# Two hybrid decoder layers: the gate and up products of the feed-forward past column 512 with the weights stationary and all tokens moving

## The chip, the core and the metric

The kernel runs on one core of a Trainium2 chip. The metric is the device time of one execution in microseconds (us). A time "at" a point of the program is counted from the start of the profiled span.

TensorE multiplies a stationary operand (`lhsT`, at most 128 by 128, brought in by a LDWEIGHTS instruction, PEld in the profile) by a moving one (`rhs`, here 128 rows and up to 512 columns) and adds into a PSUM bank. The result's partitions are the stationary operand's columns, its free dimension is the moving operand's columns. So which of the two operands is stationary decides how the result lies.

## The reference

A trunk of two layers over 256 tokens of width 1024, float32. Each layer is feed-forward, three causal mixers side by side, feed-forward:

```python
def swiglu(h, w_gate, w_up, w_down):
    return (jax.nn.silu(h @ w_gate) * (h @ w_up)) @ w_down
...
x = x + 0.5 * swiglu(rms_norm(x, ffn_norm[l, 0]), ...)   # D_MODEL 1024, D_FF 2816
...
x = x + jnp.concatenate([ya, yb, yc], axis=-1) @ w_out[l]
x = x + 0.5 * swiglu(rms_norm(x, ffn_norm[l, 1]), ...)
```

The change touches the four feed-forwards alone, and in them the way from the normed input to the hidden activations `silu(gate) * up`.

## The kernel before

**Numbers.** A product in float32 is made of three matmuls in TensorE's float32r type. Each factor is split in two parts that add up to it: `hi` (a cast on ScalarE, L173 for weights, L194 for activations) and `lo` (the rest, a subtraction on VectorE, L174 and L195). `mm3` (L187 to L191) adds x_hi*w_hi, x_hi*w_lo and x_lo*w_hi.

**Weights** come from HBM in units of 128 x 1024 float32 (512 KB): `unit` issues the DMA on SP's queue into one of 3 `raw` buffers, then makes `hi` and `lo`, of which there are 7 buffers each. For a block of 512 columns a unit holds two of the eight slices of 128 input features (k), so gate and up take four units each. For 256 columns a unit holds four slices.

**One feed-forward** (`ffn`, L255). `norm` is called once for each tile of 128 tokens: it scales x by the norm's weight, transposes it on TensorE (L225) and splits it into `xh` and `xl` (features on partitions, 8 slices k, 256 tokens). The tokens' factors `rs[t]` (one number per token, its power taken on GpSimd, L219) are not multiplied in there but left for the products. Then a loop goes over the 2816 columns in five blocks of 512 and one of 256. In a block, for each token tile t, the 128 tokens are stationary and the weights move: 24 matmuls into `pg`, 24 into `pu`, each [128 tokens x 512 features] in its own PSUM bank. ScalarE makes `sg = silu(rs*pg)` (L286), VectorE `sg = (rs*pu)*sg` (L287). Since the next product needs features on partitions, `late()` transposes `sg` on TensorE, four times 128 by 128 (two times in the last block; L293), and splits the result into `hth` and `htl`. `late()` of one token tile is called between the gate and the up products of the next.

**The down product** (`down`, L229) has the hidden activations stationary and w_down moving, in 22 steps of 12 matmuls over four PSUM banks. It adds to x (L253); its last four steps go tile by tile so that the next norm can begin.

**What sets the order.** The code is written as one stream; the Tile framework schedules each engine's instructions, so that an instruction may stand before others that the code has earlier. In each engine's queue the order is fixed. PSUM's eight banks are shared by all tiles. The first feed-forward, the mixers of layer 0, two feed-forwards, the mixers of layer 1 and the last feed-forward follow each other. In the mixers, `proj_f` (L306) already multiplies with weights stationary: 128 features stationary, the 256 tokens moving (L314 to L316).

Of the kernel before, what the change touches and what calls it, by code (L numbers as in the profile page):

```python
# [10 lines left out]
F32 = mybir.dt.float32  # L11
# [5 lines left out]
L = 256  # L17
# [22 lines left out]
# columns of the constants  # L40
# [9 lines left out]
# columns of a layer's small parameters  # L50
# [55 lines left out]
class K:  # L106
    def __init__(self, ctx, tc, I, out):
# [9 lines left out]
        per = self.cp.tile([128, 2 * D + NC_CONST + 2 * L + 128], F32, name="per")  # L117
# [4 lines left out]
        self.zero = per[:, o + 2 * L:]  # L122
# [38 lines left out]
    # ---- weights: float32 as two parts that add up to it exactly  # L161
# [35 lines left out]
    # ---- norm and transpose: x[t] -> xn^T as two parts  # L197
# [7 lines left out]
    # defer: the tokens' factors are left for the products (returned)  # L205
# [48 lines left out]

    def ffn(self, l, f):  # L255
# [4 lines left out]
        rs = [self.norm(0, prep, True)]  # L260
        first = self.units([wg[:512, 0:512]], 4, 2)
        if l == 0 and f == 0:
            self.load(1)
        rs.append(self.norm(1, prep, True))
        hh, hl = [], []
        late = lambda: None
        for c0 in range(0, FF, 512):
            cw = min(512, FF - c0)
            nb = cw // 128
            per = 1024 // cw  # L270
            ug = self.units([wg[:, c0:c0 + cw]], 8, per) if c0 else first + self.units([wg[512:, 0:512]], 4, 2)
            uu = self.units([wu[:, c0:c0 + cw]], 8, per)
            ht = self.s4([4, L], "hth", F32R)
            lt = self.s4([4, L], "htl", F32R)
            hh.append(ht)
            hl.append(lt)
            for t in range(2):
                ts = slice(t * 128, (t + 1) * 128)
                pg, pu = self.mm()[:, :cw], self.mm()[:, :cw]
# [10 lines left out]
                def late(nb=nb, cw=cw, ts=ts, sg=sg, ht=ht, lt=lt):  # L290
                    tp = self.tp()
                    for b in range(nb):
                        T.transpose(tp[:, b * 128:(b + 1) * 128], sg[:, b * 128:(b + 1) * 128], self.ident)  # L293
                    self.split(ht[:, :nb, ts], lt[:, :nb, ts], tp[:, :cw].rearrange("p (k c) -> p k c", k=nb))
# [6 lines left out]
        self.down(lhs, wd, range(FF // 128), 0.5, late)  # L301

    # ---- w_in: columns c0:c0+n, features on partitions, all tokens
# [15 lines left out]
    # the second half of the tokens is normed when first needed  # L319
# [5 lines left out]
    # tokens on partitions  # L325
# [14 lines left out]
    # ---- (I + low)^-1 of eight heads, by blocks; lts: low^T[s, h, t] of four heads each; res: the inverses' transposes  # L340
    def inverse(self, lts, res):
# [38 lines left out]
        # 32 -> 64  # L380
# [21 lines left out]
        # 64 -> 128  # L402
# [15 lines left out]
    # (I + low) W = R, four heads  # L418
# [8 lines left out]
    # y[tokens, n*128] -> columns k0.. of the two parts of y^T  # L427
# [9 lines left out]
    def rwkv(self, l, w, xn):  # L437
# [4 lines left out]
        def pre():  # L442
# [58 lines left out]
            # cumulative log decay, centred within each tile  # L501
# [13 lines left out]
            # keys  # L515
# [639 lines left out]
```

## Time and profile before

| | us |
|---|---|
| device time, median of 3 runs | 1194.26 |
| lowest and highest of them | 1193.89, 1194.32 |
| span of the profiled execution, first to last instruction | 1192.2 |
| busy in it: PE, DVE, ACT | 1139.2, 720.7, 559.3 |
| mean granted clock of TensorE, share of full speed | 0.974 |

No time of the profiled execution other than its span is given; the 2.1 us between the span and the median lie around it. How to read the rows: a matmul's duration on PE holds its way through the array, and matmuls overlap, so what a matmul takes of PE is the distance from one start to the next, not its duration. The busy time of PE counts overlaps once. A row that ends in `[0.50 <-ACT hi L173]` says that the engine was idle for 0.50 us before it, and what ended that. "x2" at a row's end means two instructions merged into one row.

### The profile page before, as it was taken

Reading aid. Unit: us, or ns where it says so; the run is one execution under the profiler, and the core shown is the slowest. Engines: PE = TensorE matmul, PEld = TensorE weight load, DVE = VectorE, ACT = ScalarE, POOL = GpSimd, SP = SyncE. Lnnn points to the kernel's source line nnn. Section 1 sums busy time; section 2 is a strip of 40 time slices with the busy share of each in tenths; the row PEclk is TensorE's granted clock in tenths of the full one; section 3 lists DMA queues with packets and bytes.
Section 4 is the critical chain, followed back from the end, with each engine's and each line's share of the span. In section 5 each row is a group of like instructions: output and inputs, shape, how many; then the busy total and the mean of one; then the engine's idle time right before and its main releaser. Section 6 shows DMA issues by size and latency. Waiting matters only on the chain. (4 is left out here: it accounts for less than half of the span.)

```text
span 1192.2 us, 20036 instructions
## 1 busy us (share of the span) xinstructions
PE 1139.2 (96%) x8100; PEld 947.5 (79%) x8100; DVE 720.7 (60%) x1206; ACT 559.3 (47%) x859; POOL 103.7 (9%) x136
## 2 busy tenths in 40 slices
PE   6999999998889999999999999999987999999998
PEld 5778887896678887888887878879866888888887
DVE  5554645689865745555465456457989366554642
ACT  5444544574463544444344445346743544443531
POOL 1000000114312100000000000001233020000000
PEclk9999999999969999999999999999999699999999
DMA  8666765652210365667646657655412105666661
GB/s 285 186 189 189 209 199 144 181 162 72 74 38 20 114 193 164 189 192 232 183 135 190 181 162 243 195 149 165 140 55 74 37 19 144 187 194 182 197 198 64
DMA packets 96988, 182.59 MB, mean 153 GB/s; under 512 B 9856, under 2 KB 36608, under 8 KB 96896
## 3 DMA queue, kind: packets, MB, share of 16 engines
q1 hardware_dynamic: 96752, 181.25, 50.9%
q8 instruction: 63, 1.03, 0.3%
q14 instruction: 29, 0.24, 0.1%
q10 hardware_dynamic: 144, 0.07, 0.0%
HBM read 180.25 MB, written 1.05 MB: 152 GB/s over the span
## 5 line engine op out<-in xcount | busy, mean ns | idle before, releaser
L174 DVE TENSOR_TENSOR lo<-raw,hi 128x1024 fp32r<-128x1024 f32 (+2 forms) x332 | 407.2, 1230 | 333.0 <-ACT hi L173 318.5
L173 ACT CAST hi<-raw 128x1024 fp32r<-128x1024 f32 (+2 forms) x332 | 346.9, 1047 | 405.2 <-PE mm L191 231.1
L189 PE MATMUL mm<-hi,xh 128*128 128x512 f32 (+2 forms) x896 | 338.2, 381 | 1.2 <-ACT xh L194 0.7
L191 PE MATMUL mm<-hi,xl 128*128 128x512 f32 (+2 forms) x896 | 337.3, 376 | 2.0 <-DVE xl L195 2.0
L190 PE MATMUL mm<-lo,xh 128*128 128x512 f32 (+2 forms) x896 | 338.0, 377 | 0.9 <-DVE lo L174 0.9
L190 PEld LDWEIGHTS mm<-lo,xh 128*128 128x128 f32 x896 | 170.4, 190 | 36.4 <-DVE lo L174 6.8
L191 PEld LDWEIGHTS mm<-hi,xl 128*128 128x128 f32 x896 | 170.1, 190 | 34.4 <-DVE xl L195 3.4
L189 PEld LDWEIGHTS mm<-hi,xh 128*128 128x128 f32 x896 | 168.7, 190 | 35.5 <-ACT hi L173 4.5
L189 PE MATMUL mm<-hi,hth 128*128 128x512 f32 x352 | 139.1, 395 | 0.0
L190 PE MATMUL mm<-lo,hth 128*128 128x512 f32 x352 | 138.7, 394 | 0.0
L191 PE MATMUL mm<-hi,htl 128*128 128x512 f32 x352 | 138.4, 393 | 0.0
L191 PEld LDWEIGHTS mm<-hi,htl 128*128 128x128 f32 x352 | 66.1, 188 | 15.6
L189 PEld LDWEIGHTS mm<-hi,hth 128*128 128x128 f32 x352 | 66.1, 188 | 15.2
L190 PEld LDWEIGHTS mm<-lo,hth 128*128 128x128 f32 x352 | 66.1, 188 | 15.0
L315 PE MATMUL mm<-xl,hi 128*128 128x256 f32 x208 | 59.3, 285 | 0.2 <-DVE xl L195 0.2
L314 PE MATMUL mm<-xh,hi 128*128 128x256 f32 x208 | 59.0, 284 | 0.1
L316 PE MATMUL mm<-xh,lo 128*128 128x256 f32 x208 | 58.9, 283 | 0.0
L219 POOL TENSOR_TENSOR ss<-ss,per 128x1 f32<-128x1 f32 x12 | 10.3, 857 | 516.0 <-DVE ss L218 502.1
L286 ACT ACTIVATE sg<-mm,ss 128x512 f32<-128x512 f32 (+1 forms) x48 | 31.3, 653 | 26.2 <-PE mm L191 26.2
L195 DVE TENSOR_TENSOR htl<-tp,hth 128x512 fp32r<-128x512 f32 (+1 forms) x48 | 31.0, 645 | 17.9 <-ACT hth L194 17.9
L314 PEld LDWEIGHTS mm<-xh,hi 128*128 128x128 f32 x208 | 39.7, 191 | 0.9 <-ACT xh L194 0.5
L315 PEld LDWEIGHTS mm<-xl,hi 128*128 128x128 f32 x208 | 39.9, 192 | 0.6 <-DVE xl L195 0.6
(314 smaller groups left out, 1220.3 us busy)
## 6 DMA issues: line engine op xcount, KB each, us to landing
raw<-in_ffn_w_gate SPq DMA_DIRECT2D x88, 512.0 KB, 4.5
raw<-in_ffn_w_up SPq DMA_DIRECT2D x88, 512.0 KB, 4.5
raw<-in_ffn_w_down SPq DMA_DIRECT2D x88, 512.0 KB, 4.2
raw<-in_w_in SPq DMA_DIRECT2D x46, 512.0 KB, 3.9
raw<-in_w_out SPq DMA_DIRECT2D x16, 512.0 KB, 3.6
gb<-in_ffn_norm SPq DMA_DIRECT2D x4, 512.0 KB, 3.9
raw<-in_w_in SPq DMA_DIRECT2D x4, 384.0 KB, 3.4
pp<-in_params SPq DMA_DIRECT2D x2, 729.5 KB, 4.8
```

The costliest lines, as they stand in the source:

```text
L173: self.A.copy(hi[:, :n], raw[:, :n])
L174: self.V.tensor_tensor(lo[:, :n], raw[:, :n], hi[:, :n].bitcast(F32), op=OP.subtract)
L189: T.matmul(ps, lhsT=x[0], rhs=w[0], start=first, stop=False)
L190: T.matmul(ps, lhsT=x[0], rhs=w[1], start=False, stop=False)
L191: T.matmul(ps, lhsT=x[1], rhs=w[0], start=False, stop=last)
L195: self.V.tensor_tensor(lo, src, hi.bitcast(F32), op=OP.subtract)
L219: G.tensor_tensor(ss[:, 3:4], ss[:, 2:3], self.c("pwr")[:, 0:1], op=OP.pow)
L286: A.activation(sg, pg, AF.Silu, scale=rs[t])
L314: T.matmul(o, lhsT=h, rhs=xh[:, k, :], start=k == 0, stop=False)
L315: T.matmul(o, lhsT=h, rhs=xl[:, k, :], start=False, stop=False)
L316: T.matmul(o, lhsT=l, rhs=xh[:, k, :], start=False, stop=k == 7)
```

## The change

Block 0 (the first 512 columns) keeps tokens stationary, but its four groups of 24 matmuls come in another order: gate for tile 0 and tile 1, then up for tile 0 and tile 1 (before: gate and up for tile 0, then for tile 1). Its two `late()` are called after the gate products of block 1.

From block 1 on, 128 columns of the weights are stationary and all 256 tokens move. A PSUM bank holds two groups of 128 features by 256 tokens; a block of 512 has two banks for gate and two for up. Gate runs over all of its four units, then up over its four. The result has features on partitions, as the down product needs it, so nothing is transposed there. But the tokens' factors lie along the free dimension now: `spread` makes them a tile `rsb` [128 x 256] with the same row in each partition, by two plain float32 matmuls of a 128 x 128 matrix of ones with a diagonal of the factors (`dg`). VectorE multiplies both gate banks by it into `gr`, ScalarE takes silu in place, VectorE multiplies both up banks into `ur`, then `ur` by `gr`, and `ur` is split into `hth` and `htl`. The `late()` that `down` gets does nothing.

The core of the diff (the rest takes comment lines out and makes room for the matrix of ones):

```diff
+    def spread(self, rs):
+        V, T = self.V, self.T
+        ps = self.tp()
+        for t in range(2):
+            dg = self.sm([128], "dg")
+            V.tensor_scalar(dg, self.ident, rs[t], None, op0=OP.mult)
+            T.matmul(ps[:, t * 128:(t + 1) * 128], lhsT=self.ones, rhs=dg, start=True, stop=True)
+        rb = self.sm([L], "rsb")
+        self.A.copy(rb, ps[:, :L])
+        return rb
...
-        for c0 in range(0, FF, 512):
...
+        h0, l0 = hold()
+        acc = {}
+        for i, us in enumerate((ug, None)):
+            us = us or self.units([wu[:, 0:512]], 8, 2)
+            for t in range(2):
+                ps = acc[i, t] = self.mm()
+                for k in range(8):
+                    self.mm3(ps, (xh[:, k, t * 128:(t + 1) * 128], xl[:, k, t * 128:(t + 1) * 128]), us[k], k == 0, k == 7)
+            if i == 0:
+                rb = self.spread(rs)
...
+        lates = [turn(0), turn(1)]
+        for c0 in range(512, FF, 512):
...
-                for ps, u in ((pg, ug), (pu, uu)):
-                    for k in range(8):
-                        self.mm3(ps, (xh[:, k, ts], xl[:, k, ts]), u[k], k == 0, k == 7)
-                    if ps is pg:
-                        late()
-                sg = self.sm([512], "sg")[:, :cw]
-                A.activation(sg, pg, AF.Silu, scale=rs[t])
-                V.scalar_tensor_tensor(sg, pu, rs[t], sg, op0=OP.mult, op1=OP.mult)
...
+            for i, w in enumerate((wg, wu)):
+                us = self.units([w[:, c0:c0 + cw]], 8, 1024 // cw)
+                pp = [self.mm() for _ in range(nb // 2)]
+                acc.append(pp)
+                for k in range(8):
+                    for b in range(nb):
+                        o = pp[b // 2][:, (b % 2) * L:(b % 2 + 1) * L]
+                        h, lo = [p[:, b * 128:(b + 1) * 128] for p in us[k]]
...
+                        mm(h, xh, True)
+                        mm(h, xl, False)
+                        mm(lo, xh, False)
+                if i == 0:
+                    for late in lates:
+                        late()
...
+                for q, ps in enumerate(pp):
...
+                    V.tensor_tensor(two(g[q]), two(ps), rb[:, None, :].to_broadcast([128, 2, L]), op=OP.mult)
+                    if i == 0:
+                        A.activation(g[q], g[q], AF.Silu)
+                        sg.append(g[q])
+                    else:
+                        V.tensor_tensor(g[q], g[q], sg[q], op=OP.mult)
+                        self.split(ht[:, 2 * q:2 * q + 2, :], lt[:, 2 * q:2 * q + 2, :], two(g[q]))
```

**How it moves instructions.** In the mixers and in the down products each engine's order is the same in both kernels, but for the load of the next norm's weights on SP's queue, which stands three weight units later. Three places in the feed-forward differ. In the rows, the number behind a name tells one buffer from another.

PE, before, at the end of a group of gate products and the start of the up products (`mm_509` and `mm_510` are the gate and up banks of token tile 0 in block 2, `hi_479` and `hi_485` weight units, `tp_535` the transposes of the tile before):

```order
L191 MATMUL mm_509<-hi_479,xl_76 128x512
L189 MATMUL mm_509<-hi_479,xh_75 128x512
L190 MATMUL mm_509<-lo_480,xh_75 128x512
L191 MATMUL mm_509<-hi_479,xl_76 128x512
L293 MATMUL tp_535<-per_70,sg_456 128x128 x4
L189 MATMUL mm_510<-hi_485,xh_75 128x512
L190 MATMUL mm_510<-lo_486,xh_75 128x512
L191 MATMUL mm_510<-hi_485,xl_76 128x512
```

These four transposes stand between the two groups of 24. PE, after, at the same kind of place in block 1 (`mm_318` and `mm_319` are the two gate banks, `mm_460` the first up bank; `sg_286` and `sg_289` belong to block 0):

```order
L328 MATMUL mm_319<-xl_77,hi_314 128x256
L328 MATMUL mm_319<-xh_76,lo_315 128x256
L328 MATMUL mm_319<-xh_76,hi_314 128x256
L328 MATMUL mm_319<-xl_77,hi_314 128x256
L328 MATMUL mm_319<-xh_76,lo_315 128x256
L310 MATMUL tp_416<-per_70,sg_286 128x128 x4
L310 MATMUL tp_423<-per_70,sg_289 128x128 x4
L328 MATMUL mm_460<-xh_76,hi_438 128x256
L328 MATMUL mm_460<-xl_77,hi_438 128x256
```

Such transposes stood at each of these places; now the eight of block 0 stand here and no others follow. A feed-forward had 44 on PE and has 8. The 1536 matmuls of 512 columns in blocks 1 to 4 of the four feed-forwards are 3072 of 256.

PE, before, where token tile 0 needs its last up unit (`hi_503`, the eighth of the block) while the gate products of tile 1 (`mm_569`) use the first ones again:

```order
L190 MATMUL mm_569<-lo_468,xh_75 128x512
L191 MATMUL mm_569<-hi_467,xl_76 128x512
L189 MATMUL mm_510<-hi_503,xh_75 128x512
L189 MATMUL mm_569<-hi_473,xh_75 128x512
L190 MATMUL mm_569<-lo_474,xh_75 128x512
L191 MATMUL mm_569<-hi_473,xl_76 128x512
L189 MATMUL mm_569<-hi_473,xh_75 128x512
L190 MATMUL mm_510<-lo_504,xh_75 128x512
L191 MATMUL mm_510<-hi_503,xl_76 128x512
L189 MATMUL mm_510<-hi_503,xh_75 128x512
L190 MATMUL mm_510<-lo_504,xh_75 128x512
```

The first product with `hi_503` stands five matmuls ahead of the second. PE, after, where one unit of a block gives way to the next:

```order
L328 MATMUL mm_319<-xh_76,hi_296 128x256
L328 MATMUL mm_319<-xl_77,hi_296 128x256
L328 MATMUL mm_319<-xh_76,lo_297 128x256
L328 MATMUL mm_318<-xh_76,hi_302 128x256
L328 MATMUL mm_318<-xl_77,hi_302 128x256
L328 MATMUL mm_318<-xh_76,lo_303 128x256
L328 MATMUL mm_318<-xh_76,hi_302 128x256
L328 MATMUL mm_318<-xl_77,hi_302 128x256
```

Before, a block needs its eight units twice with seven buffers, and the scheduler set the last up unit's products in between those of the next tile. After, a unit is used in one run of 24 matmuls and is then free.

DVE, before, one and a half token tiles of blocks 1 and 2 (`lo` splits weight units, `sg` is the product with the up bank, `htl` the split of the transposed tile):

```order
L287 SCALAR_TENSOR_TENSOR sg_396<-mm_340,ss_79,sg_396 128x512
L174 TENSOR_TENSOR lo_468<-raw_465,hi_467 128x1024
L195 TENSOR_TENSOR htl_338<-tp_425,hth_337 128x4x128
L174 TENSOR_TENSOR lo_474<-raw_471,hi_473 128x1024
L174 TENSOR_TENSOR lo_480<-raw_477,hi_479 128x1024
L174 TENSOR_TENSOR lo_486<-raw_483,hi_485 128x1024
L287 SCALAR_TENSOR_TENSOR sg_456<-mm_400,ss_116,sg_456 128x512
L174 TENSOR_TENSOR lo_492<-raw_489,hi_491 128x1024
L174 TENSOR_TENSOR lo_498<-raw_495,hi_497 128x1024
L195 TENSOR_TENSOR htl_338<-tp_535,hth_337 128x4x128
L174 TENSOR_TENSOR lo_504<-raw_501,hi_503 128x1024
```

One instruction on a result stands between every one to three weight splits. DVE, after, from within the up products of block 1 to the gate products of block 2 (`mm_460` and `mm_461` are up banks of block 1, `mm_594` the first gate bank of block 2):

```order
L175 TENSOR_TENSOR lo_701<-raw_698,hi_700 128x1024
L175 TENSOR_TENSOR lo_707<-raw_704,hi_706 128x1024
L341 TENSOR_TENSOR ur_558<-mm_460,rsb_210 128x512
L341 TENSOR_TENSOR ur_559<-mm_461,rsb_210 128x512
L346 TENSOR_TENSOR ur_558<-ur_558,gr_430 128x512
L346 TENSOR_TENSOR ur_559<-ur_559,gr_431 128x512
L175 TENSOR_TENSOR lo_713<-raw_710,hi_712 128x1024
L196 TENSOR_TENSOR htl_293<-ur_558,hth_292 128x512
L196 TENSOR_TENSOR htl_293<-ur_559,hth_292 128x512
L175 TENSOR_TENSOR lo_719<-raw_716,hi_718 128x1024
L175 TENSOR_TENSOR lo_835<-raw_832,hi_834 128x1024
L175 TENSOR_TENSOR lo_841<-raw_838,hi_840 128x1024
L341 TENSOR_TENSOR gr_692<-mm_594,rsb_210 128x512
```

The work on a block's result stood in four places and stands in two, up to four instructions in a row between two weight splits. Further, VectorE has the two `dg` of a feed-forward: the first right behind the first tile's sums of squares, ahead of a weight split or of an update of x, the second behind five weight splits. PE has the two matmuls of `spread` right behind the gate products of block 0 and four matmuls later.

## Rows read from the trace of the kernel before

**Rows 1.** The page, part 1 (busy time, share of the span, instructions) and part 2 (the granted clock in 40 slices), of the whole program.

```profile
PE 1139.2 (96%) x8100; PEld 947.5 (79%) x8100; DVE 720.7 (60%) x1206; ACT 559.3 (47%) x859; POOL 103.7 (9%) x136
...
PEclk9999999999969999999999999999999699999999
```

**Rows 2.** The stretches view: busy time of PE, PEld, DVE, ACT and POOL (us, instructions), granted clock of TensorE, DMA share and GB/s, for the first feed-forward, the mixers of layer 0 and the second feed-forward.

```profile
0.00:206.00 206.00, 196.97 (x905) 159.22 (x906) 109.13 (x115) 94.82 (x114) 3.95 (x13) 1.00 0.67 201
206.00:411.00 205.00, 182.57 (x2246) 158.93 (x2245) 152.67 (x391) 105.09 (x224) 46.59 (x57) 0.93 0.32 95
411.00:603.00 192.00, 192.00 (x906) 156.77 (x905) 104.62 (x108) 87.78 (x104) 2.02 (x2) 1.00 0.61 184
```

**Rows 3.** The waits view of PE over the whole program: who was waited for, us in total, times, the longest.

```profile
PE mm L191 <- DVE xl L195: 2.0, 2, 1.0
...
PE mm L190 <- DVE lo L174: 0.9, 2, 0.5
```

**Rows 4.** The stretches view, one block of 512 features of the first feed-forward, from one point of the loop to the same point of the next block; columns as in Rows 2.

```profile
79.85:103.21 23.36, 23.36 (x105) 18.65 (x104) 12.47 (x13) 10.48 (x13) 0.00 (x0) 1.00 0.63 183
```

**Rows 5.** The order of time on PE in that feed-forward (start us, duration us, line, operation, out<-in, count): the first and the last of 47 matmuls of 512 columns that follow each other.

```profile
56.48 0.39 PE L190 MATMUL mm<-lo,xh 128*128 128x512 f32 x1
...
67.19 0.39 PE L191 MATMUL mm<-hi,xl 128*128 128x512 f32 x1
```

**Rows 6.** The same view around four transposes of a 512-wide block, from the matmul before them to the second one behind them.

```profile
32.21 0.40 PE L191 MATMUL mm<-hi,xl 128*128 128x512 f32 x1
32.45 0.60 PE L293 MATMUL tp<-per,sg 128*128 128x128 f32 x4
...
33.12 0.39 PE L190 MATMUL mm<-lo,xh 128*128 128x512 f32 x1
```

**Rows 7.** The same view where matmuls of the next token tile stand between those of a 512-wide block: the first and the last of eight matmuls.

```profile
98.03 0.40 PE L191 MATMUL mm<-hi,xl 128*128 128x512 f32 x1
...
99.80 0.39 PE L191 MATMUL mm<-hi,xl 128*128 128x512 f32 x1
```

**Rows 8.** The same view, matmuls with 256 moving columns: first and last of 66 in a row of w_in (L314 to L316), of 46 there, of 45 in the last block of a feed-forward, of 23 in that of the second feed-forward.

```profile
223.95 0.28 PE L315 MATMUL mm<-xl,hi 128*128 128x256 f32 x1
...
231.54 0.28 PE L314 MATMUL mm<-xh,hi 128*128 128x256 f32 x1
...
215.10 0.28 PE L316 MATMUL mm<-xh,lo 128*128 128x256 f32 x1
...
220.44 0.27 PE L316 MATMUL mm<-xh,lo 128*128 128x256 f32 x1
...
135.62 0.28 PE L191 MATMUL mm<-hi,xl 128*128 128x256 f32 x1
...
140.85 0.28 PE L190 MATMUL mm<-lo,xh 128*128 128x256 f32 x1
...
538.25 0.28 PE L190 MATMUL mm<-lo,xh 128*128 128x256 f32 x1
...
540.89 0.28 PE L191 MATMUL mm<-hi,xl 128*128 128x256 f32 x1
```

**Rows 9.** The weight loads (PEld) under the matmuls of the second of those runs.

```profile
216.05 0.19 PEld L316 LDWEIGHTS mm<-xh,lo 128*128 128x128 f32 x1
216.17 0.19 PEld L314 LDWEIGHTS mm<-xh,hi 128*128 128x128 f32 x1
```

**Rows 10.** The order of time on PE in the mixers: eight records of plain float32 matmuls of 128 by 128, two records each, and what follows.

```profile
369.09 0.39 PE L608 MATMUL tp<-vt,kbt 128*128 128x128 f32 x2
...
369.98 0.22 PE L837 MATMUL tp<-gW,mg 128*128 128x64 f32 x1
```

**Rows 11.** The start of the program in order of time: the first tile's factor on POOL, the first weight split on DVE; on PE, some 13 us after its first matmul, a stretch of six matmuls with two waits for weights, of which the first, the fourth and the last are shown.

```profile
8.43 0.55 POOL L219 TENSOR_TENSOR ss<-ss,per 128x1 f32<-128x1 f32 x1 [7.50 <-DVE ss L218]
...
9.09 1.23 DVE L174 TENSOR_TENSOR lo<-raw,hi 128x1024 fp32r<-128x1024 f32 x1 [0.75 <-ACT hi L173]
...
22.04 0.40 PE L191 MATMUL mm<-hi,xl 128*128 128x512 f32 x1
...
24.20 0.50 PE L190 MATMUL mm<-lo,xh 128*128 128x512 f32 x1 [0.54 <-DVE lo L174]
...
24.77 0.40 PE L189 MATMUL mm<-hi,xh 128*128 128x512 f32 x1
```

**Rows 12.** Groups of instructions on DVE, shapes kept apart: count, busy us, mean ns, idle before.

```profile
L174 DVE TENSOR_TENSOR lo<-raw,hi 128x1024 fp32r<-128x1024 f32 x326 | 400.7, 1232 | 324.2 <-ACT hi L173 309.6 <-PE mm L190 13.2
L287 DVE SCALAR_TENSOR_TENSOR sg<-mm,ss,sg 128x512 f32<-128x512 f32 x40 | 29.9, 748 | 4.7 <-PE mm L191 3.4
L195 DVE TENSOR_TENSOR htl<-tp,hth 128x512 fp32r<-128x512 f32 x40 | 27.6, 691 | 17.9 <-ACT hth L194 17.9
...
L216 DVE TENSOR_TENSOR xn<-per,gb 128x512 f32<-128x512 f32 x16 | 10.9, 689 | 7.0 <-DMA gb<-in_ffn_norm 6.7
```

**Rows 13.** The hand-over into the third feed-forward, in order of time: on PE the first matmul, on DVE the last piece of the second token tile's transposed input; before it, on POOL, the first tile's factor, and the next instruction on DVE.

```profile
603.69 0.50 PE L189 MATMUL mm<-hi,xh 128*128 128x512 f32 x1
...
607.34 0.68 DVE L195 TENSOR_TENSOR xl<-tp,xh 128x512 fp32r<-128x512 f32 x1
...
598.82 0.55 POOL L219 TENSOR_TENSOR ss<-ss,per 128x1 f32<-128x1 f32 x1 [182.58 <-DVE ss L218]
...
599.81 0.69 DVE L253 SCALAR_TENSOR_TENSOR per<-mm,per 128x512 f32<-128x512 f32 x1 [1.13 <-PE mm L191]
```

More of the change, by code (lines that the diff above doesn't have):

```diff
@@ L121, in __init__ @@
         self.vfirst = per[:, o:o + 2 * L].rearrange("p (b t) -> p b t", b=2)
-        self.zero = per[:, o + 2 * L:]
+        self.zero, self.ones = [per[:, o + 2 * L + i * 128:o + 2 * L + (i + 1) * 128] for i in range(2)]
+        nc.gpsimd.memset(self.ones, 1.0)
         self.pp = {}
@@ L259, in ffn @@
         wg, wu, wd = I["ffn_w_gate"][l, f], I["ffn_w_up"][l, f], I["ffn_w_down"][l, f]
-        rs = [self.norm(0, prep, True)]
-        first = self.units([wg[:512, 0:512]], 4, 2)
+        rs = [None, None]
+        rs[0] = self.norm(0, prep, True)
+        ug = self.units([wg[:512, 0:512]], 4, 2)
         if l == 0 and f == 0:
             self.load(1)
-        rs.append(self.norm(1, prep, True))
+        rs[1] = self.norm(1, prep, True)
+        ug += self.units([wg[512:, 0:512]], 4, 2)
         hh, hl = [], []
-        late = lambda: None
@@ new lines, in turn, with late @@
+        def turn(t):
+            ts = slice(t * 128, (t + 1) * 128)
+            sg = self.sm([512], "sg")
+            A.activation(sg, acc[0, t], AF.Silu, scale=rs[t])
+            V.scalar_tensor_tensor(sg, acc[1, t], rs[t], sg, op0=OP.mult, op1=OP.mult)
+            def late():
+                tp = self.tp()
+                for b in range(4):
+                    T.transpose(tp[:, b * 128:(b + 1) * 128], sg[:, b * 128:(b + 1) * 128], self.ident)
+                self.split(h0[:, :, ts], l0[:, :, ts], tp.rearrange("p (k c) -> p k c", k=4))
+            return late
@@ new lines, in ffn @@
+            ht, lt = hold()
+            acc = []
+            for i, w in enumerate((wg, wu)):
[6 more added lines that the diff above has]
+                        h, lo = [p[:, b * 128:(b + 1) * 128] for p in us[k]]
+                        mm = lambda a, c, s: T.matmul(o, lhsT=a, rhs=c[:, k, :], start=s and k == 0 and b % 2 == 0,
+                                                      stop=k == 7, skip_group_check=True)
+                        mm(h, xh, True)
[3 more added lines that the diff above has]
+                    for late in lates:
+                        late()
+                    lates = []
+                    sg = []
+                g = [self.sm([512], "gu"[i] + "r") for _ in pp]
+                for q, ps in enumerate(pp):
+                    two = lambda ap: ap.rearrange("p (b t) -> p b t", b=2)
+                    V.tensor_tensor(two(g[q]), two(ps), rb[:, None, :].to_broadcast([128, 2, L]), op=OP.mult)
[5 more added lines that the diff above has]
+                        self.split(ht[:, 2 * q:2 * q + 2, :], lt[:, 2 * q:2 * q + 2, :], two(g[q]))
@@ L299, in lhs @@
             return hh[c][:, b, ts], hl[c][:, b, ts]
-        self.down(lhs, wd, range(FF // 128), 0.5, late)
+        self.down(lhs, wd, range(FF // 128), 0.5, lambda: None)
     def proj_f(self, w, c0, n, xn, sink):
```

21 lines of the change are left out of this document (5 added, 16 removed).

## The prediction

> **What bounds the kernel now.** I read the busy times and the granted clock first. PE is busy for 1139.2 of 1192.2 us, DVE for 720.7, ACT for 559.3, and TensorE has its full clock outside the mixers [rows 1]. [...] PE's waits for activations and weight parts in matmuls come to 2 or 3 us in the whole program [rows 3]. So a feed-forward lasts as long as its list of PE instructions, and the change is priced by what it does to that list. One block of 512 columns takes 23.36 us, with DVE busy for 12.47 and ACT for 10.48 of them [rows 4].
>
> The unit of the sum is the distance from start to start. Matmuls of 512 columns follow each other at (67.19 - 56.48) / 46 = 0.2328 us [rows 5]. The 96 of a block are then 22.35 us. With four transposes set in, two distances take 0.91 us and not 0.47, so the four cost 0.44, or 0.11 each [rows 6]; eight in a block are 0.88. That leaves 23.36 - 22.35 - 0.88 = 0.13 us, and it is found at one place: seven distances where the next tile's matmuls are set in between take 1.77 us and not 1.63, 0.14 more [rows 7].
>
> **The change, part by part.** The sum is made on the profiled execution (span 1192.2) and applied to the median, 1194.26, which lies 2.1 us above it; that rest is start and end of the program, and nothing there changes.
>
> *Transposes removed.* 36 of 44 in each feed-forward, 144 in all, at 0.11 us: **-15.8 us**. Each stood in PE's queue between matmuls that were ready, so all of it lies on the path. Bounds: none is hidden, so the error is that of the row, 0.5 us.
>
> *512 columns become 2 x 256.* 1536 matmuls become 3072; columns and products are the same, weight loads double. The form itself, 128 features stationary and 256 tokens moving, is in the trace at w_in: (231.54 - 223.95) / 65 = 0.1168 us and (220.44 - 215.10) / 45 = 0.1187. Tokens stationary and 256 weight columns moving, in the very place the change is made, gives (140.85 - 135.62) / 44 = 0.1189 and, in a shorter run, (540.89 - 538.25) / 22 = 0.1200 [rows 8]. The two kinds differ by less than the runs of each. I take 0.1180, between the two w_in runs and a little to the slower one's side, since that is the same form: a pair costs 0.2360 for 0.2328, so 1536 x 0.0032 = **+4.9 us**. Bounds: 0.1168 gives +1.2, 0.1200 gives +11.1. The last block was 256 wide already and stays so.
>
> The load is hidden in these rows: loads of 0.19 us start 0.12 us apart, each under a running matmul of 256 columns [rows 9]. [...]
>
> *Spread.* Two plain float32 matmuls of 128 by 128 per feed-forward. In the mixers four such take 0.89 us, 0.22 each [rows 10]: 8 x 0.22 = **+1.8 us**. If each also breaks the stream as in rows 7, 0.14 more, +2.9. Their inputs come early. The second `dg` stands behind five weight splits on DVE and its matmul behind 52 others, 12 us after the feed-forward's first.
>
> *The interleaved unit.* Now each unit is used in one run, so the 0.14 us per block goes, in 16 blocks: **-2.2 us**. Bounds: 0, if new waits for weights cost the same, and -2.8, if the four first blocks lose theirs as well. The order of the first block still has such a place, so I don't count them.
>
> *Start of the program.* Weights come late there: six matmuls take 24.77 - 22.04 = 2.73 us where five distances are 1.16, so 1.57 us are lost to two waits for an up unit [rows 11]. In the new order gate runs for both tiles first, 48 matmuls on the same four units, and the up units are needed some 5 us later than now. Both waits go. Against it, `dg` of the first tile now stands ahead of the first weight split and waits for GpSimd's power, which ends at 8.98; the split began at 9.09 [rows 11], so it moves by some 0.2 (an estimate: `dg`'s own length less the 0.1 between). **-1.4 us**, bounds 0 and -2.0.
>
> *Work beside PE.* Per block of 512, DVE loses two products with the up bank (0.75 each) and two splits (0.69), and gains four products from PSUM, two products in SBUF and two splits. Taking 0.69 to 0.75 for each, from the nearest rows [rows 12], that is +2.8 us, so 15.3 of some 22.7. The tightest half is the gate phase (11.3 us): two products of the block before with up, two of up with gate, two splits and four weight splits at 1.23 make 9.1. PE covers it. What is queued behind the instructions that wait for PE are weight splits, and by the order at least six of the seven buffers' splits stand ahead of each wait. ACT has 44 silus and 44 casts of results for 48 and 48, and four small copies. Nothing, therefore: **0**. The last block's results are needed after 20 steps of the down product, 20 x 12 x 0.23 = 56 us later.
>
> *The norm at the hand-over.* Tile 1 of the input is needed after 24 matmuls, not 48. The third feed-forward starts at 603.69 us; 24 matmuls and four transposes take it to 609.8, and the last piece of tile 1 is there at 608.0 [rows 13]. So 1.8 us are in hand, and **0** is charged; if it were late by 1 us, three hand-overs would cost 3. The first tile's `dg` waits for GpSimd's power, over at 599.37, and the update of x behind it starts at 599.81: covered too. SP's order changes only in that one small load of norm weights goes three units later in the down product, long before it is used.
>
> *Mixers.* Not touched. Their granted clock can fall a little earlier or later against their work; two such stretches, so I allow 2 us to either side and charge 0.
>
> Sum: -15.8 + 4.9 + 1.8 - 2.2 - 1.4 = **-12.7 us**, from 1194.3 to **1181.6 us**, 1.1% faster.
>
> **The rivals.**
> First, the 256-wide matmul is slower in a long stream than in the short runs. All else is -17.6 us, so the gain is gone when 3072 matmuls each cost 5.7 ns over 116.4, at a distance of 0.1221 us. For it: the feed-forward's own runs are the slowest of the four, up to 0.1200, and none lasts longer than 8 us where the new stream lasts 100. Against it: the spread of runs shows no growth with length, the longest is the fastest. At 0.1200 the time is 1187.8; at 0.125, 1203. Slower than before: 4%; between 1188 and that: 6%, half of it within 0.2% of before.
> Second, DVE becomes the bound of the gate phase. Its products read PSUM and a broadcast operand, a form that the trace doesn't have. From 11.3 us on, that is when the four products there take over 1.25 us each and not 0.7, PE waits for weight splits; at 1.5 us each the excess is 1.0 us in 16 blocks, and the gain is gone: 1198. Against it: 512 columns out of PSUM with a second operand are 0.69 to 0.75 in all rows. 3%.
> Third, weight loads that don't overlap, by rows' 0.19 us for each of 1536 more: 1474. The rows of w_in speak against it. 1%. [...]
> Fourth, the transposes cost nothing, because PE was waiting for something else meanwhile: then +3.1 remains, 1197. The stretch of 23.36 us that adds up without a wait speaks against it. 1%.
> That the change doesn't do what it says is excluded by the order: 144 transposes less and 3072 matmuls of 256 stand in it.
>
> **How the numbers follow.** The forecast, 1177 to 1188, has 85%. With all bounds on the good side (+1.2, +1.8, -2.8, -2.0, mixers -2) it is 1174.7, with cadence at its worst and no gain from the order 1191. The range 1176 to 1190 leaves out the tails of both and the four rivals. A measurement tells about 0.2% (2.4 us) from no change: faster 0.85 + 0.03 = 0.88, same 0.03, slower 0.04 + 0.03 + 0.01 + 0.01 = 0.09.
>
> **What would show it.** In the profile after: L328's matmuls 0.117 to 0.119 us apart with weight loads under them; a block at 22.6 to 22.8 us, DVE busy in it for about 15; 32 transposes of `sg` at L310; no wait of PE for `hi` or `lo` beyond the first 25 us; the mixers as before. A block above 23.3 us, or a distance of 0.122, would make the forecast wrong, and so would a PE that waits for `lo` while DVE stands at `ur` or `gr`.

## Result and profile after

The changed kernel takes 1182.69 us (median of 4 runs, 1182.12 to 1183.9) against 1194.29 for the one before: a ratio of 0.99, 95% interval 0.9886 to 0.9914. The profiled execution spans 1180.3 us, at a mean granted clock of 0.975.

The page of the changed kernel, parts 1 and 2, answers to [rows 1]:

```profile
PE 1123.4 (95%) x9508; PEld 1006.5 (85%) x9508; DVE 759.3 (64%) x1278; ACT 560.2 (47%) x855; POOL 106.0 (9%) x137
...
PEclk9999999999869999999999999999998699999999
```

PE has 1408 instructions more and is busy for 15.8 us less; DVE is busy for 38.6 us more, and the kernel is faster all the same. The stretches view of the changed kernel, each feed-forward from the norm's first transpose (the first from the start) to its first matmul of the down product; columns as in [rows 2]:

```profile
0.00:139.87 139.87, 130.71 (x988) 124.57 (x989) 89.18 (x102) 71.16 (x86) 4.70 (x12) 1.00 0.72 219
405.98:533.69 127.71, 127.05 (x990) 122.01 (x988) 82.76 (x93) 63.74 (x75) 1.47 (x1) 1.00 0.64 190
594.90:723.47 128.57, 127.15 (x990) 122.08 (x989) 83.07 (x93) 62.64 (x74) 3.99 (x5) 1.00 0.63 188
987.03:1115.36 128.33, 127.89 (x990) 122.81 (x989) 82.91 (x93) 63.13 (x74) 1.47 (x1) 1.00 0.64 189
```

The same view of the kernel before has PE busy for the whole of the last three:

```profile
410.82:541.01 130.19, 130.19 (x635) 106.61 (x634) 73.67 (x76) 63.73 (x76) 1.47 (x1) 1.00 0.62 183
602.39:732.59 130.20, 130.20 (x635) 106.61 (x634) 73.68 (x76) 61.87 (x75) 3.10 (x5) 1.00 0.62 183
997.22:1127.03 129.81, 129.81 (x635) 106.93 (x634) 73.31 (x76) 63.04 (x76) 1.47 (x1) 1.00 0.60 180
```

Now it is idle for 0.66, 1.42 and 0.44 us there. The same stretches and those of the mixers (from the norm's first transpose to the first matmul with w_out), read in the profiled execution of each kernel of this study:

| kernel | first feed-forward | the other three | sum of four | mixers, layer 0 and 1 |
|---|---|---|---|---|
| before | 144.12 | 130.19, 130.20, 129.81 | 534.3 | 172.8, 170.8 |
| changed | 139.87 | 127.71, 128.57, 128.33 | 524.5 | 172.6, 170.0 |
| e1_spread_later | 139.86 | 127.12, 127.20, 127.76 | 521.9 | 173.2, 171.3 |
| e2_no_factors | 139.03 | 126.45, 126.55, 127.12 | 519.2 | 173.9, 172.1 |
| e3_transposes_back | 144.03 | 131.79, 131.65, 132.27 | 539.7 | 172.3, 169.5 |
| e4_block0_order_only | 141.58 | 130.22, 130.33, 129.99 | 532.1 | 172.4, 170.5 |
| e5_block0_old_order | 143.00 | 128.26, 128.01, 127.51 | 526.8 | 172.6, 170.0 |
| e6_more_on_vector | 139.36 | 127.49, 128.37, 128.24 | 523.5 | 173.0, 171.9 |
| e7_eight_buffers_before | 143.75 | 129.94, 130.09, 129.86 | 533.6 | 182.7, 174.2 |
| e8_diag_on_gpsimd | 139.02 | 126.77, 126.87, 127.65 | 520.3 | 174.1, 169.1 |
| e9_changed_again | 139.56 | 127.62, 128.85, 129.02 | 525.1 | 173.5, 172.3 |
| e10_fewer_activation_buffers | 145.03 | 130.17, 130.81, 129.81 | 535.8 | 173.3, 171.2 |
| e11_all_blocks_256 | 145.47 | 131.98, 132.05, 131.29 | 540.8 | 173.0, 171.7 |

Of the 11.8 us between the two spans, 9.8 lie in the four feed-forwards up to the down product, 0.8 in the down products (the last block's transposes stood there) and 1.1 in the mixers. Two executions of the same kernel, changed and e9_changed_again, differ by up to 0.7 us in a feed-forward and by 3.3 in the mixers together. The kernel before and e10_fewer_activation_buffers, whose PE order is the same up to the mixers of layer 0, differ by 0.9 in the first feed-forward. So feed-forwards are compared by these sums; the mixers tell nothing below 3 us, and the first feed-forward alone nothing below 1.

**The stream.** The order of time on PE in the first feed-forward of the changed kernel, first and last of 767 matmuls of 256 columns that follow each other, and the weight loads under two of them:

```profile
49.62 0.28 PE L328 MATMUL mm<-xl,hi 128*128 128x256 f32 x1
...
139.75 0.28 PE L328 MATMUL mm<-xh,lo 128*128 128x256 f32 x1
```
```profile
72.23 0.19 PEld L328 LDWEIGHTS mm<-xh,lo 128*128 128x128 f32 x1
72.34 0.19 PEld L328 LDWEIGHTS mm<-xh,hi 128*128 128x128 f32 x1
```

90.13 / 766 = 0.1177 us from start to start, over the up products of block 1 and blocks 2 to 5. The same stretch of the other three feed-forwards gives 0.1169, 0.1170 and 0.1179. With the runs of gate products of block 1, 3444 distances have a mean of 0.1174. Loads of 0.19 us start 0.11 to 0.12 apart, under running matmuls, as in [rows 9].

The stretches view of one block of the changed kernel, 192 matmuls of the first feed-forward, answers to [rows 4]:

```profile
72.20:94.75 22.55, 22.55 (x194) 22.55 (x193) 15.24 (x18) 10.67 (x12) 0.00 (x0) 1.00 0.72 205
```

23.36 us became 22.55, PE is never idle, and DVE is busy for 15.24: the forecast had 22.6 to 22.8 and 15.3. The groups on DVE, columns as in [rows 12]:

```profile
L341 DVE TENSOR_TENSOR ur<-mm,rsb 128x512 f32<-128x512 f32 x36 | 24.3, 687 | 2.5 <-PE mm L328 2.4
L341 DVE TENSOR_TENSOR gr<-mm,rsb 128x512 f32<-128x512 f32 x36 | 24.2, 687 | 1.0 <-PE mm L328 1.0
...
L346 DVE TENSOR_TENSOR ur<-ur,gr 128x512 f32<-128x512 f32 x36 | 23.3, 683 | 0.1
```

A product of PSUM with the broadcast factors takes 687 ns, like the forms that the trace before had (691 and 748 there).

**What was not forecast.** The waits of PE for feed-forward tiles in the changed kernel, columns as in [rows 3]:

```profile
PE tp L263 <- DVE dg L262: 3.9, 4, 1.4
PE mm L192 <- DVE xl L196: 2.0, 2, 1.0
PE mm L190 <- ACT xh L195: 0.7, 3, 0.3
```

The wait for `lo` of [rows 3] is gone; four waits for `dg` are new. The order of time around that of the third feed-forward, on POOL, ACT, DVE and PE:

```profile
598.94 1.40 POOL L220 TENSOR_TENSOR ss<-ss,per 128x1 f32<-128x1 f32 x1 [7.12 <-DMA raw<-in_ffn_w_up]
...
607.49 1.05 ACT L174 CAST hi<-raw 128x1024 fp32r<-128x1024 f32 x1 [2.23 <-DMA raw<-in_ffn_w_gate]
608.78 1.05 ACT L174 CAST hi<-raw 128x1024 fp32r<-128x1024 f32 x1 [0.24 <-DMA raw<-in_ffn_w_gate]
...
608.57 2.52 DVE L175 TENSOR_TENSOR lo<-raw,hi 128x1024 fp32r<-128x1024 f32 x2 [2.05 <-ACT hi L174]
611.01 0.28 DVE L262 TENSOR_SCALAR dg<-per,ss 128x128 f32<-128x128 f32 x1
...
609.53 0.40 PE L192 MATMUL mm<-hi,xl 128*128 128x512 f32 x1
611.35 0.49 PE L263 MATMUL tp<-dg,per 128*128 128x128 f32 x2 [1.42 <-DVE dg L262]
611.59 0.48 PE L190 MATMUL mm<-hi,xh 128*128 128x512 f32 x1
```

The factor that `dg` is made of is there at 600.34. `dg` itself takes 0.28 us, and DVE is idle for 2.05 us just before 608.57. But `dg` stands behind two weight splits, these wait for casts, and the casts here for weights that were still on their way: it starts at 611.01, when PE could have used its result from 609.53 + 0.23 = 609.76.

### The profile page after: what moved, and what is told of

Read it like the earlier page. It is cut to its first block, busy times and chain, and to the rows that moved or that the text cites. A ratio compares the mean times of both kernels' runs of the same rounds, so it can differ in the third digit from the quotient of the medians.

```text
span 1180.3 us, 22922 instructions
## 1 busy us (share of the span) xinstructions
PE 1123.4 (95%) x9508; PEld 1006.5 (85%) x9508; DVE 759.3 (64%) x1278; ACT 560.2 (47%) x855; POOL 106.0 (9%) x137
## 5 line engine op out<-in xcount | busy, mean ns | idle before, releaser
L328 PE MATMUL mm<-xh,hi 128*128 128x256 f32 x1152 | 322.5, 280 | 0.0
L328 PE MATMUL mm<-xh,lo 128*128 128x256 f32 x1152 | 322.2, 280 | 0.0
L328 PE MATMUL mm<-xl,hi 128*128 128x256 f32 x1152 | 322.0, 280 | 0.0
L328 PEld LDWEIGHTS mm<-xh,hi 128*128 128x128 f32 x1152 | 216.9, 188 | 0.2
L328 PEld LDWEIGHTS mm<-xl,hi 128*128 128x128 f32 x1152 | 216.5, 188 | 0.2
L328 PEld LDWEIGHTS mm<-xh,lo 128*128 128x128 f32 x1152 | 216.6, 188 | 0.0
L192 PE MATMUL mm<-hi,xl 128*128 128x512 f32 (+2 forms) x256 | 99.2, 387 | 2.0 <-DVE xl L196 2.0
L190 PE MATMUL mm<-hi,xh 128*128 128x512 f32 (+2 forms) x256 | 99.1, 388 | 0.7 <-ACT xh L195 0.7
L191 PE MATMUL mm<-lo,xh 128*128 128x512 f32 (+2 forms) x256 | 98.2, 384 | 0.1
L192 PEld LDWEIGHTS mm<-hi,xl 128*128 128x128 f32 x256 | 49.6, 194 | 12.8 <-DVE xl L196 4.1
L367 PE MATMUL mm<-xh,hi 128*128 128x256 f32 x208 | 58.5, 282 | 0.2
L368 PE MATMUL mm<-xl,hi 128*128 128x256 f32 x208 | 58.6, 282 | 0.1
L369 PE MATMUL mm<-xh,lo 128*128 128x256 f32 x208 | 58.3, 280 | 0.0
```

The lines of the kernel that those rows point to most:

```text
L190: T.matmul(ps, lhsT=x[0], rhs=w[0], start=first, stop=False)
L191: T.matmul(ps, lhsT=x[0], rhs=w[1], start=False, stop=False)
L192: T.matmul(ps, lhsT=x[1], rhs=w[0], start=False, stop=last)
L328: mm = lambda a, c, s: T.matmul(o, lhsT=a, rhs=c[:, k, :], start=s and k == 0 and b % 2 == 0, stop=k == 7, skip_group_check=True)
L367: T.matmul(o, lhsT=h, rhs=xh[:, k, :], start=k == 0, stop=False)
L368: T.matmul(o, lhsT=h, rhs=xl[:, k, :], start=False, stop=False)
```

## Experiments

**The spread later, and left out.** Two edits of the changed kernel. In the first, the call stands behind the up products of block 0:

```diff
             if i == 0:
-                rb = self.spread(rs)
...
+        rb = self.spread(rs)
```

> The changed kernel with one call moved: the tokens' factors are spread (two `dg`, two matmuls) behind the up products of block 0, not behind its gate products. Theory: PE's wait for `dg` (3.9 us in the trace of the changed kernel, and some more for restarting the stream) was in the place of the call alone, so it goes: 1178.5 us, from 1177.5 to 1179.5, and no wait of PE at L263. Rival: VectorE itself is late there, behind weight splits, and PE meets the same delay as a wait for `lo` a few matmuls on: 1182 to 1183.

1181.37 us (1180.25 to 1184.43), ratio to before 0.9889 (0.9872 to 0.9906), above the expected range. The feed-forwards gave 2.5 us. Three of the four waits went. In the first feed-forward the scheduler moved the second `dg` back too, and PE waits for it there:

```profile
PE tp L263 <- DVE dg L262: 1.2, 1, 1.2
```

The time alone does not tell this from the changed kernel, since the mixers took 2 us more.

```diff
-                rb = self.spread(rs)
+                rb = self.sm([L], "rsb")
+                self.G.memset(rb, 1.0)
```

> The changed kernel without `spread`: the tile that multiplies gate and up past column 512 holds ones, so the norm's factors of the tokens are left out there. Theory: `spread` costs its four records of PE per feed-forward (1.8 us in all, as the prediction has it) and the wait for `dg` (3.9 us or a little more): 1176.5 to 1177. Rival: the wait hid something else that PE then meets, and only the 1.8 us go: 1180.9.

1177.13 us (1176.71 to 1180.15), 0.9857 (0.9841 to 0.9872); the feed-forwards 5.3 us less than the changed kernel's. The spread cost that much (5.9 against the second execution of the changed kernel), and 1.8 were forecast. One wait for a weight, of 0.5 us, stands in its first feed-forward, which the changed kernel does not have.

**`dg` on GpSimd.** The same spread, its matmuls in the same place, but no `dg` in VectorE's queue; each is made right behind the power of its token tile:

```diff
+        def diag(t):
+            dgs[t] = self.sm([128], "dg")
+            self.G.tensor_tensor(dgs[t], self.ident, rs[t].to_broadcast([128, 128]), op=OP.mult)
```

It ran with the changed kernel beside it on one chip.

> Changed kernel with the diagonals dg made on GpSimd, each right behind the power that ends its token tile's factor, so that no dg stands in VectorE's queue; the matmuls of the spread stay behind the gate products of block 0. Theory (what the spread cost beyond its records is the second dg standing on VectorE behind weight splits that wait for buffers): the four waits of TensorE for dg, about 4.8 us in all, go, and no other wait appears in the first blocks: 1177.5 to 1178.5 us, with the feed-forwards at 139, 126.9, 127.0 and 127.6 us up to their down product. Rival (the wait is in the nature of the first block: without dg TensorE waits there for a weight split, or GpSimd has the diagonals ready too late): 1182 to 1183, with a wait for lo or dg of the same size in the rows.

> The changed kernel once more, unaltered, beside the others on one chip: 1182.7 us as before. Its mixers against those of its first run show how much two runs of the same instructions differ there: theory 1 to 2 us; rival: they agree within 0.3, and the 2 us by which the spread-later kernel's mixers differed were its own doing.

1179.79 us (1179.12 to 1180.24), 0.9876 (0.9864 to 0.9889), against 1185.1 (1182.22 to 1185.99), 0.9913 (0.99 to 0.9926), for the unaltered one. The feed-forwards are 4.7 us shorter than those of the unaltered one beside it and 4.2 shorter than in its first execution, where 4.8 us of waits were expected to go; their sum, 520.3, is close to the 520.5 expected. The two times lie 5.3 us apart, and both above what was expected, by 1.3 and 2.4; their mixers differ by 2.6. PE, at the place shown above:

```profile
607.73 0.39 PE L192 MATMUL mm<-hi,xl 128*128 128x512 f32 x1
607.96 0.60 PE L261 MATMUL tp<-dg,per 128*128 128x128 f32 x4
608.32 0.48 PE L190 MATMUL mm<-hi,xh 128*128 128x512 f32 x1
608.63 0.39 PE L191 MATMUL mm<-lo,xh 128*128 128x512 f32 x1
```

From the last matmul ahead of the four records to the second one behind them are 0.90 us. Without them these are two distances of 0.233, so the four cost 0.43, or 0.11 each, as [rows 10] say. The sums agree with it: this kernel's feed-forwards are 1.2 us longer than those without the factors, which have the 0.5 us wait for a weight; that makes 1.7, four times 0.43. The row of `dg` on GpSimd, eight instructions with their shortest, median and longest duration in ns:

```profile
L278 POOL TENSOR_TENSOR dg<-per,ss x8: 400/401/1502, 9.0 to 989.8; 128x128 f32<-128x128 f32 x8
```

No wait took the place of those for `dg`; the rival is refuted. Of the kernels that leave nothing out it has the lowest median, though its interval overlaps that of e1_spread_later.

The unaltered kernel waits again, in the same place:

```profile
612.20 0.49 PE L263 MATMUL tp<-dg,per 128*128 128x128 f32 x2 [1.70 <-DVE dg L262]
```

**The transposes put back**, 36 for each feed-forward, of a constant, whose results nothing uses:

```diff
+                tq = self.tp()
+                for b in range(nb):
+                    T.transpose(tq[:, b * 128:(b + 1) * 128], self.ones, self.ident)
```

> The changed kernel with 36 transposes put back into each feed-forward, in groups of four (two in the last block) behind the gate and the up products of blocks 1 to 5; they transpose a constant into a bank that nobody reads. Theory of the prediction: 0.11 us of PE each, 144 of them, 15.8 us: 1198.5, from 1197 to 1200. Rival one: they were hidden, 1182.7. Rival two: each costs its whole duration of 0.272 us, 39 us: 1222.

1197.83 us (11 runs, 1194.35 to 1203.11), 1.0029 (1.0015 to 1.0042); the feed-forwards 15.3 us more, so 15.3 / 144 = 0.106 us for each. Without this term the change is a loss.

**The order of block 0.** Alone in the kernel before, whose other blocks stay as they were:

```diff
+        for i, us in enumerate((ug, None)):
+            us = us or self.units([wu[:, 0:512]], 8, 2)
+            for t in range(2):
+                ps = acc[i, t] = self.mm()
```

> The kernel before with one part of the change: block 0 runs gate for both token tiles and then up; blocks 1 to 5 stay as they were, no `spread`. Theory of the prediction: the two waits at the start of the program go (1.4 us), and perhaps the interleaved unit of four blocks (0.14 each): 1192.4 to 1193. Rival: the waits move to another unit, 1194.3; worse, up to 1196, if the second tile's norm, needed 24 matmuls earlier, holds PE at the four starts.

1191.01 us (1189.83 to 1192.15), 0.9967 (0.9956 to 0.9979). The first feed-forward gives 2.5 us, the others nothing (up to 0.2 longer). 1.4 were forecast, from two waits. The order of time on PE in the kernel before, some four us ahead of those two:

```profile
17.71 0.40 PE L189 MATMUL mm<-hi,xh 128*128 128x512 f32 x1
18.46 0.50 PE L190 MATMUL mm<-lo,xh 128*128 128x512 f32 x1 [0.35 <-DVE lo L174]
```

A third wait: the distance is 0.75 us and not 0.23, and it went too. With the interleaved unit of this block (0.14) that makes 1.57 + 0.52 + 0.14 = 2.2; the other 0.3 is within what the first feed-forward differs by.

The other way round, the old order in e1_spread_later:

```diff
-        for i, us in enumerate((ug, None)):
-            us = us or self.units([wu[:, 0:512]], 8, 2)
-            for t in range(2):
+        uu = self.units([wu[:, 0:512]], 8, 2)
+        for t in range(2):
+            for i, us in enumerate((ug, uu)):
```

> The kernel of e1 with block 0 back in the old order (gate and up for tile 0, then for tile 1); the rest as in e1. Theory: block 0's order is worth the 1.4 us at the program's start and little else: 1.4 us above e1, some 1180. Rival: the order of block 0 is worth nothing or costs, since blocks 1 and on no longer need their units twice: as e1 or up to 1 us below it.

1185.92 us (1184.51 to 1187.42), 0.9926 (0.9912 to 0.9939), 4.5 more than e1_spread_later, where 1.4 were expected; the first feed-forward is 3.1 longer, the other three 1.7 together. Waits for weights are back, five where the kernel before has three; four of them in the order of time on PE:

```profile
22.26 0.50 PE L190 MATMUL mm<-hi,xh 128*128 128x512 f32 x1 [0.51 <-ACT hi L174]
...
23.52 0.50 PE L191 MATMUL mm<-lo,xh 128*128 128x512 f32 x1 [0.52 <-DVE lo L175]
...
25.43 0.72 PE L190 MATMUL mm<-hi,xh 128*128 128x512 f32 x2 [0.48 <-ACT hi L174]
...
26.70 0.51 PE L191 MATMUL mm<-lo,xh 128*128 128x512 f32 x1 [0.54 <-DVE lo L175]
```

Not all of the 4.5 us is the order of block 0 as such. PE waits for `dg` once more in all four feed-forwards, 2.8 us in all (1.2 in e1_spread_later). And the last two waits stand in e10_fewer_activation_buffers too, at 25.54 and 26.80, with the PE order of the kernel before: in both, PE was some 0.7 to 0.8 us earlier at this place (first wait for `lo` at 17.77 and 17.64 us, and at 18.46 in the kernel before), and these two weights were not.

**More work on VectorE**: two products more, used by nothing, for each up bank.

```diff
+                        for _ in range(2):
+                            V.tensor_tensor(two(self.sm([512], "dx")), two(ps), rb[:, None, :].to_broadcast([128, 2, L]), op=OP.mult)
```

> The changed kernel with two further products of each up bank with the factors on VectorE, results unused: four more instructions of some 0.7 us in each block of 512, standing behind the up products. Theory: VectorE has slack over the whole block (15.3 of 22.6 us busy, 18.2 with these) and weight splits are six units ahead, so nothing changes: 1182.7, at most 1184. Rival, the bound as the prediction worked it out for the gate half alone (9.1 of 11.3 us, 12.0 with these): 0.7 us in each of 16 blocks, 1194.

1183.13 us (1181.03 to 1185.04), 0.99 (0.9884 to 0.9916). One block of it:

```profile
71.70:94.25 22.55, 22.55 (x194) 22.55 (x193) 17.34 (x21) 10.38 (x12) 0.00 (x0) 1.00 0.65 202
```

The same 22.55 us, with DVE busy for 2.1 more (three of the block's four added products lie in this window). VectorE is no bound of the block, and has at least that much to give.

**The interleaved unit.** The kernel before with eight weight buffers, paid for with two activation buffers, and then with those two taken away alone (the first line of this diff):

```diff
-N_1040 = 20
+N_1040 = 18
...
-BH = 7
+BH = 8
```

> The kernel before with eight buffers for weight parts and not seven (and 18 for activations, not 20): the last up unit no longer waits for a buffer, and in blocks 1 to 4 PE's order has no interleaved unit. Theory of the prediction: 0.14 us per block go, 16 to 20 blocks, 2.2 to 2.8 us: 1191.5 to 1192. Rival: those 0.14 us are a cost of something else, 1194.3.

> Kernel before with 18 activation buffers of that size for 20, and seven weight buffers as before. Theory (the 20 us that the kernel with eight weight buffers lost lie in the two activation buffers that it gave up, by waits in the mixers, while the eighth weight buffer gained some 2 us in the feed-forwards): 1214 to 1217 us, mixers 7 to 13 us longer, a block of 512 at 23.3 to 23.4 us. Rival (the eighth weight buffer itself disturbs the mixers): 1194.5.

1214.09 us (1213.79 to 1220.86), 1.0173 (1.0151 to 1.0195), and 1194.21 (12 runs), 0.9995 (0.9986 to 1.0005). One block with eight buffers:

```profile
79.85:103.06 23.21, 23.21 (x106) 18.77 (x105) 12.50 (x13) 10.62 (x13) 0.00 (x0) 1.00 0.61 182
```

23.21 for 23.36: 0.15 us here, as [rows 7] said. All 16 blocks of this kind, each from one set of transposes to the same place in the next block, take 373.35 us in the kernel before and 371.36 with eight buffers, 2.0 less. The four feed-forwards together gave only 0.7; the difference stands in their first and last blocks. The rest goes the other way too: 9.9 and 3.4 us more in the mixers, and 4.6 and 4.7 in the two products with w_out behind them. The reason expected for these, the two activation buffers, fell: without them alone the kernel loses nothing. PE's waits for `S` at one line of the mixers, with eight weight buffers and with seven, both with 18 activation buffers:

```profile
PE tp L390 <- ACT S L376: 11.7, 2, 8.6
```
```profile
PE tp L390 <- ACT S L376: 2.0, 3, 1.0
```

So the eighth weight buffer, in a kernel with 18 activation buffers, brings another order, with such waits: the stretch of the first product with w_out holds 192 instructions on PE for 170 with seven buffers, and the granted clock in the mixers of layer 0 before it is 0.86 for 0.89. Which instruction stands wrong there stays open, and eight weight buffers with 20 activation buffers were not run. The stretches view of that product, with eight and with seven:

```profile
387.98:425.02 37.04, 35.45 (x192) 28.09 (x193) 22.48 (x76) 15.51 (x38) 5.22 (x6) 1.00 0.29 92
379.74:412.14 32.40, 31.06 (x170) 25.20 (x169) 21.83 (x66) 14.60 (x36) 4.51 (x6) 1.00 0.35 105
```

**Width without the turn.** The kernel before with all blocks 256 wide, tokens stationary:

```diff
-        for c0 in range(0, FF, 512):
-            cw = min(512, FF - c0)
+        for c0 in range(0, FF, 256):
+            cw = 256
```

> Kernel before with every block of columns 256 wide and not 512, tokens stationary as before, transposes kept: the change's width alone, without its turn of the operands. Per 512 columns 192 matmuls of 256 for 96 of 512 and the same eight transposes, in more groups; four units per block, which seven buffers hold at once, so no interleaved unit. Theory (a matmul of 256 columns costs 0.1174 us in a long stream, whichever operand is stationary): 1920 pairs at 2 ns more are 4 us, the interleaved unit gives back 2 to 2.8: 1195 to 1197. Rival (the turn of the operands is what keeps the distance small): at 0.1200 a pair costs 7 ns more, 14 us in all: 1206.

1199.89 to 1201.58 us in four runs (a fifth took 2793.7 us and is left out of the ratio), 1.0054 (1.0041 to 1.0067); the feed-forwards 6.5 more than before's. The order of time on PE, from one pair of transposes to the next:

```profile
83.28 0.36 PE L189 MATMUL mm<-hi,xh 128*128 128x256 f32 x1
83.48 0.28 PE L190 MATMUL mm<-lo,xh 128*128 128x256 f32 x1
...
88.95 0.29 PE L191 MATMUL mm<-hi,xl 128*128 128x256 f32 x1
89.07 0.38 PE L294 MATMUL tp<-per,sg 128*128 128x128 f32 x2
89.21 0.37 PE L189 MATMUL mm<-hi,xh 128*128 128x256 f32 x1
89.41 0.28 PE L190 MATMUL mm<-lo,xh 128*128 128x256 f32 x1
```

5.93 us for 48 matmuls and two transposes. Over some 4000 distances the matmul takes 0.1185 us, between the theory's 0.1174 and the rival's 0.1200, so a pair costs 0.2369 - 0.2328 = 4.1 ns more than one of 512, and 1920 of them 7.9 us. The two transposes take 0.24 where four took 0.44: 1.6 us in all. With 2.8 for the interleaved unit the sum is +6.7 for 6.5 measured. With the weights stationary (0.1174) a pair costs 2.0 ns more than one of 512. So the changed stream saves half of what the width costs; it does not make 256 columns free. That the turn itself is the cause is not shown: by feed-forward the distances are 0.1187, 0.1186, 0.1186 and 0.1179 here and 0.1177, 0.1170, 0.1171 and 0.1179 in the changed kernel, so in the last one there is no difference.

## Why the prediction came out right

The time was 1182.7 for 1181.6, but three steps were mis-sized, one of them by its mechanism, and their errors met: +3.5 us on the spread, -1.8 on the narrower matmuls, -1.1 at the start.

- **Transposes, -15.8**: right. e3_transposes_back gives 15.3. The eight that remain stand in a row and cost 0.11 each.
- **512 into 2 x 256, +4.9**: right in kind, too large. 1536 x (2 x 0.1174 - 0.2328) = +3.1. The trace before had both values; the w_in run of 66 was nearer than the one of 46 that I leaned to. The first rival (slower in a long stream) is refuted by 767 matmuls in a row.
- **Spread, +1.8**: wrong, 5.3. The records were right (0.43 for a feed-forward). The step that failed is "Their inputs come early. The second `dg` stands behind five weight splits". Five splits are 6 us of work, and I took the queue for that long. It lasts as long as what the splits wait for: the first row of [rows 12] has 324 us of idle time ahead of the weight splits, 310 of it for `hi`. e8_diag_on_gpsimd shows the cause: the same spread without `dg` in that queue gives 4.2 to 4.7 us back.
- **The interleaved unit, -2.2**: right, 2.0 in the 16 blocks with eight buffers, and none of it left in the new stream (22.55 us for 192 distances of 0.1174).
- **Start, -1.4**: right in kind, too small: -2.5 by e4_block0_order_only. A third wait of that stretch was overlooked: [rows 3] counts two for `lo`, and the sum used one. PE's waits in matmuls for activations and weight parts were 4.3 us in all in the kernel before, not 2 or 3.
- **Work beside PE, 0**: right. The gate phase's 9.1 of 11.3 us was a stricter limit than there is: e6_more_on_vector put four more products of some 0.69 us into a block for nothing (22.55 us in both). Why the limit of that half did not hold was not shown. The second rival is refuted.
- **Norm at the hand-over, 0**: right; the waits for `xl` and `xh` are those of before (2.0 and 0.7 us in both). The third and the fourth rival are refuted by the stream and by e3_transposes_back.
- **Mixers, 0 within 2**: -1.1, and a second execution of the same kernel has them 3.3 longer, so nothing is to be read from it.

Measured: -15.3 + 3.1 + 5.3 - 2.0 - 2.5 = -11.4, where the medians differ by 11.6. That is closer than the parts allow. By the stages, feed-forwards and down products gave 10.7, and not all of that is the change's doing. The order of time on PE at the start, of before and of the changed kernel:

```profile
13.70 0.63 PE L191 MATMUL mm<-hi,xl 128*128 128x512 f32 x1
...
16.00 0.48 PE L191 MATMUL mm<-hi,xl 128*128 128x512 f32 x1
```
```profile
13.82 0.40 PE L192 MATMUL mm<-hi,xl 128*128 128x512 f32 x1
...
15.31 0.48 PE L192 MATMUL mm<-hi,xl 128*128 128x512 f32 x1
```

At 13.7 us a matmul lasts 0.63 us before and 0.40 after (0.42 and 0.23 from start to start), and the second execution came 0.69 us earlier to the same matmul behind the second tile's transposes. The stretches view gives a granted clock of 1.00 from 12 to 14 us in both, so the rows do not say why. It goes with the execution and not with the change: that matmul starts at 15.77 in e9_changed_again, and at 15.19 in e10_fewer_activation_buffers, which has the order of the kernel before. In e4_block0_order_only it starts at 15.96, so what is told of the start above is free of it. 11.6 + 0.7 - 10.7 = 1.6 us stay unassigned; the two executions of the changed kernel differ by 0.7 in a single feed-forward. That the sum meets the medians to 0.2 us is luck.

## What to carry to other kernels

The place of `dg` in VectorE's queue was priced by what the instructions ahead of it waited for, not by their durations (the spread cost 5.3 us for 1.8 forecast): read the idle time in front of that group before calling an input early, and put a small operand that TensorE needs on an engine whose queue holds nothing that waits at that time (4.2 to 4.7 us less here); VectorE stood idle here (for 2.05 us up to 608.57, with the factor there at 600.34), and `dg` could still not start. Where PE is busy without a gap, count its instructions and price each by the distance from start to start in a row of the same form; a layout that makes transposes needless was worth their distances here (0.106 us each), less what narrower matmuls cost (2.0 ns for each pair in place of one of 512). Look through the whole first block for waits, not for the two largest.

## What the hardware showed that I had not expected

- The distance of 256-column matmuls was 0.1185 us with tokens stationary and 0.1174 with weights, over some 4000 and 3444 distances in two kernels; in the last feed-forward it was 0.1179 in both. Why is open.
- GpSimd makes a 128 x 128 product with a broadcast column in 0.40 us, and in 1.50 in the worst of eight cases (VectorE: 0.28); it was the better place here, with 4.2 to 4.7 us less in the feed-forwards.
- A weight buffer more, with two activation buffers less, made the kernel 1.7% slower, without a further wait for weights (PE waited 0.9 us for `lo` and 0.5 for `hi`, as in the kernel before); the two activation buffers less alone cost nothing (ratio 0.9995). The order in another stage had changed.
